# Output projection of a hybrid decoder layer in two parts of K, each by seven half-size products for eight

## The chip, the cores and the metric

The kernel runs on one core of one Trainium2 chip. The metric is the device time of one execution in microseconds. The engines are TensorE (PE; its weight loads are shown apart as PEld), VectorE (DVE), ScalarE (ACT), GpSimd (POOL) and SyncE (SP), whose queue issues every DMA of this kernel.

## The reference

One layer of a hybrid decoder over 2048 tokens and 1024 channels, in float32:

```python
def hybrid_layer(x, g_pre, g_post, w_in, b_i, b_f, g_head, conv_w, g_conv, w_out):
    h = rms_norm(x, g_pre)
    proj = jnp.einsum('bsd,de->bse', h, w_in)
    q, k, v, o, z_m, i_pre, f_pre, u, gate_b, gate_c, z_c = jnp.split(proj, _split_points(), axis=-1)
    ...
    hm = mlstm_chunkwise(qh, kh, vh, log_i, log_f)
    hm = group_rms_norm(hm, g_head, N_MLSTM_HEADS, x.dtype)
    y_m = jax.nn.silu(z_m) * jax.nn.sigmoid(o) * hm
    conv = causal_depthwise_conv(gate_c * u, conv_w)
    y_c = jax.nn.silu(z_c) * group_rms_norm(gate_b * conv, g_conv, N_CONV_GROUPS, x.dtype)
    mix = jnp.concatenate([y_m, y_c], axis=-1)
    out = jnp.einsum('bse,ed->bsd', mix, w_out)
    return x + rms_norm(out, g_post)
```

`mix` has 2048 columns, 1024 of the mLSTM heads and 1024 of the convolution; `w_out` is 2048 x 1024.

## The kernel before

The sequence is worked in two halves (hf = 0, 1) of 1024 tokens. Every float32 matmul is made of three fp32r matmuls: an operand is split into a high part (a cast on ScalarE, line 185) and a remainder (a subtraction on VectorE, line 188).

**Input projections.** The output columns come in 32 pairs of 128-column blocks (`PAIRS`). A pair, times two groups of 512 tokens, times two halves of K (the reduction axis, 2 x 512), is a 2 x 2 by 2 x 2 block product, and `pair` (line 444) does it with seven products instead of eight. Each product is 4 x 3 = 12 matmuls of 128 x 512 (`mm_prod`, lines 296 to 298). The seven right-hand operands of a half ("hops": sums and differences of quarters of the normalised input, each split in two) stay in SBUF; the left-hand ones (sums and differences of weight quarters) stream by. The products accumulate in the PSUM banks X, D and Y; `evac` (line 452) copies X to Y after product 0, and `take` hands the four finished quarters to the stage's own work.

**Slots.** A slot is one product. `on(slot, fn, level)` puts work into a slot; `run_slot` issues it behind the slot's matmuls, in the order of the levels EVAC, WEIGHT, STORE, OTHER, and `in_order` fixes the order of every engine. For a product in slot s the raw weights are loaded in slot s-8, summed on VectorE in s-5, cast on ScalarE in s-4, their remainder taken on VectorE in s-3. The first half ends at slot U = 224, the second at 2U. The mLSTM, convolution and gate work is spread over the same slots.

**Change of operands at U.** During the first half's last block of pairs, `hop_make` computes the second half's operands and stores them in DRAM (`hop_scr`). `plan_fill` (line 1154) then loads them in 14 pieces of 512 KB through four staging tiles (`hop_fill`), and casts and subtracts them into the same SBUF tiles (`hop_high`, `hop_low`) from slot U-6 on, four of the loads from U-10 on. Product j of the new half can only start when its operand is there.

**Output projection.** After slot 2U (first instruction at line 1207) there are no slots. For each of the 16 tiles of 128 tokens the 16 blocks of K are accumulated into two PSUM banks of 512 output columns, with `w_out` in SBUF (28 pieces put into the hop tiles at the end of the second half by `plan_wo`, four more into a pool of their own). The token tile's operand is loaded, multiplied (h from the mLSTM by the gate g, line 1111) and split one tile ahead. The two banks are squared and summed on ScalarE (line 1228), multiplied by `g_post` on VectorE (line 1229), scaled by the row's 1/rms and added to x (line 1238), and stored. The last tile is cut into 512, 256 and 256 columns, done one after the other.

Pools take buffers in turn: a tile that gets the buffer of an earlier one waits for that one's last reader, a DMA too.

Of the kernel before, what the change touches and what calls it, by code (L numbers as in the profile page):

```python
# [29 lines left out]
NPAIR = 32  # L30
NG = NC // 2
# [32 lines left out]
def hybrid_layer_kernel(  # L64
# [54 lines left out]
    w_scr = dram.tile([NPAIR, 4, P, Q], F32, name="w_scr")  # L119

# [90 lines left out]
    def run_slot():  # L211
        while agenda[clock[0]]:
# [227 lines left out]

    def bank_(name):
        return pps.tile([P, Q], F32, tag="pp", name=name)

    def pair(hf, n):
        kind, i = PAIRS[n]
# [3 lines left out]
        def take(ch, qd, src, psum=False):  # L449
            TAKE[kind](hf, i, ch, qd, src, psum)  # L450
# [376 lines left out]
    def hop_fill(m):  # L827
# [4 lines left out]
        nc.sync.dma_start(t, hop_scr[j][:, ks, :])  # L832
        return j, ks, t

    def hop_high(m):
        j, ks, t = S["fill", m]
        if m % 2 == 0:
            S["next", j] = (hop_tile(j, "H", f"hH{j}"), hop_tile(j, "L", f"hL{j}"))
        split_h(S["next", j][0][:, ks], t)

    def hop_low(m):
        j, ks, t = S.pop(("fill", m))
        H, L = S["next", j]
# [3 lines left out]
    def start():  # L847
# [65 lines left out]
        def fill(j, b):  # L913
            H, L = hops[j] = hop_tile(j, "H", f"hH{j}"), hop_tile(j, "L", f"hL{j}")
# [135 lines left out]
    NE = 16  # L1050
    NT = SEQ // P
    wos, ys = {}, {}

    def wo_raw(e, half, raw=None):
        raw = raw or t5("wor")
        nc.sync.dma_start(raw, wout[e * P : (e + 1) * P, seg(half)])
        return raw

    def wo_split(e, half, w2, raw):
        split(w2[:, 0, seg(half)], w2[:, 1, seg(half)], raw)  # L1060
        wos[e] = (w2[:, 0], w2[:, 1])

    def load_wo(e, w2):
        for half in range(2):
            wo_split(e, half, w2, wo_raw(e, half))

    def plan_wo(e):
        s = 2 * U - NPROD + 1 + 3 * e // 4
        j, part = divmod(e, 2)
        R = {}  # L1070

        def load():
            for half in range(2):
                R[half] = wo_raw(e, half, rawp.tile([P, Q], F32, tag="raw", name="wor"))

        def go():
            w2 = hpool.tile([P, 2, DM], F32R, tag=f"h{j}{'HL'[part]}", name="wo")
            for half in range(2):
                wo_split(e, half, w2, R[half])

        on(s - 2, load)
        on(s, go)

    def y_parts(t, tile_):

        hf, tt = divmod(t, NC)
        ts = slice(tt * P, (tt + 1) * P)
        ys[t] = []
        for g in range(2):
            R = {}  # L1090
            for half in range(2):
                es = slice(4 * half, 4 * half + 4)

                def load(g=g, half=half, es=es, R=R):
                    r = R[half] = tpool.tile([P, 4, P], F32, tag="t5", name="yr")
                    if g == 0:
                        for i in range(2):
                            nc.sync.dma_start(
                                r[:, 2 * i : 2 * i + 2, :],
                                h_scr[hf][2 * half + i, tt].rearrange("e p t -> p e t"))  # L1100
                        R["g", half] = tpool.tile([P, 4, P], F32, tag="t5", name="gr")
                        nc.sync.dma_start(R["g", half], g_scr[hf][es, :, ts].rearrange("e p t -> p e t"))
                    else:
                        nc.sync.dma_start(r, y_scr[hf][es, :, ts].rearrange("e p t -> p e t"))

                def go(g=g, half=half, es=es, R=R):
                    if half == 0:
                        R["H"], R["L"] = tile_(f"yH{g}"), tile_(f"yL{g}")
                    r = R[half]
                    if g == 0:  # L1110
                        nc.vector.tensor_tensor(r, r, R["g", half], ALU.mult)
                    split(R["H"][:, es], R["L"][:, es], r)
                    if half == 1:
                        ys[t].extend((R["H"][:, i, :], R["L"][:, i, :]) for i in range(8))

                yield load, go

    def load_y(t, tile_):
        for load, go in y_parts(t, tile_):
            load()  # L1120
            go()

    def even_tile():
        tags = iter(("cv", "cv", "cu", "rb"))
        return lambda name: c4(next(tags), name, [P, 8, P], F32R)

    def y_even(t):
        load_y(t, even_tile())
# [10 lines left out]
    ml = ph1.enter_context(tc.tile_pool(name="ml", bufs=1, reuse_waits="tile"))  # L1139
# [14 lines left out]
    def plan_fill():  # L1154
        for m in range(2 * NPROD):
            s = U - 6 + 11 * m // 14
            early = U - 10 if m < 4 else U - 6 + 11 * (m - 4) // 14 + 2
            def load(m=m):
                S["fill", m] = hop_fill(m)
            on(early, load)  # L1160
            on(s, lambda m=m: hop_high(m))
            on(s + 1, lambda m=m: hop_low(m))

    plan_fill()
    for i, (load, go) in enumerate(y_parts(0, even_tile())):
        on(2 * U - 3 * NPROD + 2 * i, load)
        on(2 * U - 3 * NPROD + 2 * i + 3, go)
    for e in range(2 * NPROD):
        plan_wo(e)
# [4 lines left out]
    class Next(dict):  # L1174
        def __missing__(self, j):
            return S["next", j]

    hops = Next()
    for n in range(NPAIR):
        pair(1, n)  # L1180
        if n == 0:
            for qd, terms in enumerate((((0, 0), (3, 1)), ((0, 0), (4, 0), (6, 1)))):
                bank = gate_proj([(hops[j], lo) for j, lo in terms])
                later(0, lambda qd=qd, bank=bank: gate_take(1, qd, bank))
    while any(agenda.values()):
        run_slot()
    in_order()
    ph1.close()


    def pool2(name, **kw):
        return ctx.enter_context(tc.tile_pool(name=name, reuse_waits="tile", **kw))

    op = pool2("op", bufs=2)
    wo = pool2("wo", bufs=2)
    po = pool2("po", bufs=6, space=PSUM)

    def y_odd(t):
        load_y(t, lambda name: wp.tile([P, 8, P], F32R, tag="w", name=name))

    with tc.high_priority(offset=150):
        for e in range(2 * NPROD, NE):
            load_wo(e, wo.tile([P, 2, DM], F32R, tag="wo", name="wo"))
        y_odd(1)
    gpost = op.tile([P, DM], F32, tag="gpost", name="gpost", bufs=1)
    nc.sync.dma_start(gpost, g_post.broadcast_to([P, DM]))
    for t in range(NT):
        if 0 < t < NT - 1:
            (y_odd if t % 2 == 0 else y_even)(t + 1)
        y2 = ys.pop(t)  # L1210
        xr = op.tile([P, DM], F32, tag="xr", name="xr")
        nc.sync.dma_start(xr, x[t * P : (t + 1) * P, :])
        last = t == NT - 1
        cuts = (0, 512, 768, 1024) if last else (0, 512, 1024)
        parts = [slice(c0, c1) for c0, c1 in zip(cuts, cuts[1:])]
        pts = [po.tile([P, 512], F32, tag="po", name="po")[:, : sl.stop - sl.start] for sl in parts]
        order = [(e, i) for e in range(NE) for i in range(len(parts))]
        if last:
            order.sort(key=lambda ei: ei[1])
# [3 lines left out]
        ot = op.tile([P, DM], F32, tag="ot", name="ot")  # L1223
        junk = op.tile([P, DM], F32, tag="junk", name="junk", bufs=1)
        sss = []
# [67 lines left out]
```

## Time and profile before

| | us |
|---|---|
| median of three runs | 1746.16 |
| lowest and highest run | 1745.42, 1746.17 |
| the profiled execution | 1746.06 |
| its span, first to last instruction | 1744.3 |

The profile is one execution. "Busy" of PE counts a matmul from start to its modelled end, and matmuls overlap; how fast they follow one another is read from their starts. `w` is a split left-hand operand, `wraw` its raw form, `hH` and `hL` the two parts of a right-hand one, `hst` its staging tile, `po` an output bank, `yr` and `yH`, `yL` a token tile and its parts, `ot` the finished rows.

### The profile page before, as it was taken

The page shows a single profiled execution, that of the slowest core. Times are in us where ns is not written, and L with a number is a line of the kernel's source. Part 1 is how long each engine was busy: PE and PEld are TensorE (multiplying, and loading weights), DVE is VectorE, ACT ScalarE, POOL GpSimd, SP SyncE. Part 2 cuts the span into 40 slices and gives each one's busy share as a digit, 9 for nine tenths or more (in the row PEclk, how much of TensorE's full clock was granted, in tenths as well). Part 3 has the DMA queues.
Part 4 walks back from the last instruction along what each step waited for, and adds up shares of the span by engine and source line. Part 5 has one row for each costly group of instructions (what it writes and reads, how often), then busy time and mean ns, then how long its engine had stood idle before and what let it go on. Part 6 is the DMA issues. An engine that isn't in the chain of part 4 may idle for free.

```text
span 1744.3 us, 23010 instructions
## 1 busy us (share of the span) xinstructions
PE 1699.0 (97%) x7773; PEld 1406.4 (81%) x7773; DVE 1152.0 (66%) x2175; ACT 821.4 (47%) x1608; POOL 121.8 (7%) x120
## 2 busy tenths in 40 slices
PE   6799999999999999999999999999999999999998
PEld 4578887888888888788888888888888878888887
DVE  7887669798979888846557777777656753333221
ACT  6244456555656655634445556555656631111110
POOL 5000002010202000000001010102000000000000
PEclk9889999999999999999999999999999999999999
DMA  4177764555455698757774545463556784333310
GB/s 158 50 185 197 186 198 148 159 159 184 150 160 169 210 276 279 247 136 182 177 180 112 160 121 148 106 178 110 154 145 176 235 261 148 120 117 118 110 47 31
DMA packets 360488, 278.40 MB, mean 160 GB/s; under 512 B 188233, under 2 KB 270417, under 8 KB 360370
## 3 DMA queue, kind: packets, MB, share of 16 engines
q1 hardware_dynamic: 360370, 276.93, 55.1%
q8 instruction: 61, 1.00, 0.2%
q14 instruction: 57, 0.47, 0.1%
HBM read 183.25 MB, written 93.59 MB: 159 GB/s over the span
## 4 chain that ended last, share of the span: by engine, by line
PE 87%; DVE 7%; DMA 3%; ACT 1%; issue 1%; SPq 0%; DVEq 0%; ACTq 0%
PE uY L296 9%; PE uY L298 9%; PE uY L297 9%; PE po L624 7%; PE po L623 6%; PE po L625 6%; PE uX L298 6%; PE uX L296 6%; PE uX L297 6%; PE uD L296 6%; PE uD L298 6%; PE uD L297 6%; DMA wor<-in_wout_dram 1%; PE gate L497 1%; PE num L625 1%
## 5 line engine op out<-in xcount | busy, mean ns | idle before, releaser
L185 ACT CAST w<-wraw 128x512 fp32r<-128x512 f32 x410 | 254.2, 621 | 221.0 <-PE uY L298 94.5
L188 DVE TENSOR_TENSOR w<-wraw,w 128x512 fp32r<-128x512 f32 x410 | 279.9, 686 | 81.7 <-ACT w L185 81.4
L296 PE MATMUL uY<-hH,w 128*128 128x512 f32 x744 | 292.6, 393 | 6.9 <-ACT uY L455 4.7
L298 PE MATMUL uY<-hH,w 128*128 128x512 f32 x744 | 290.8, 391 | 0.0
L297 PE MATMUL uY<-hL,w 128*128 128x512 f32 x744 | 290.5, 391 | 0.0
L623 PE MATMUL po<-wo,yH 128*128 128x512 f32 (+1 forms) x528 | 203.3, 385 | 2.2 <-ACT wo L185 2.2
L624 PE MATMUL po<-wo,yH 128*128 128x512 f32 (+1 forms) x528 | 204.5, 387 | 0.2 <-DVE wo L188 0.2
L625 PE MATMUL po<-wo,yL 128*128 128x512 f32 (+1 forms) x528 | 203.1, 385 | 0.0
L296 PE MATMUL uX<-hH,w 128*128 128x512 f32 x496 | 195.4, 394 | 5.0 <-ACT w L185 5.0
L298 PE MATMUL uX<-hH,w 128*128 128x512 f32 x496 | 194.6, 392 | 4.2 <-DVE w L188 4.2
L296 PE MATMUL uD<-hH,w 128*128 128x512 f32 x496 | 194.6, 392 | 0.0
L297 PE MATMUL uX<-hL,w 128*128 128x512 f32 x496 | 194.1, 391 | 0.0
L298 PE MATMUL uD<-hH,w 128*128 128x512 f32 x496 | 193.6, 390 | 0.0
L297 PE MATMUL uD<-hL,w 128*128 128x512 f32 x496 | 193.5, 390 | 0.0
L296 PEld LDWEIGHTS uY<-hH,w 128*128 128x128 f32 x744 | 140.0, 188 | 37.4 <-ACT uY L455 6.1
L298 PEld LDWEIGHTS uY<-hH,w 128*128 128x128 f32 x744 | 140.1, 188 | 29.8
L297 PEld LDWEIGHTS uY<-hL,w 128*128 128x128 f32 x744 | 140.1, 188 | 28.2 <-DVE hL L188 0.2
L623 PEld LDWEIGHTS po<-wo,yH 128*128 128x128 f32 x528 | 99.5, 188 | 23.6 <-ACT wo L185 2.6
L624 PEld LDWEIGHTS po<-wo,yH 128*128 128x128 f32 x528 | 99.6, 189 | 21.2 <-DVE wo L188 1.2
L625 PEld LDWEIGHTS po<-wo,yL 128*128 128x128 f32 x528 | 99.7, 189 | 20.3
L298 PEld LDWEIGHTS uX<-hH,w 128*128 128x128 f32 x496 | 93.6, 189 | 24.8 <-DVE w L188 4.9
L296 PEld LDWEIGHTS uX<-hH,w 128*128 128x128 f32 x496 | 93.8, 189 | 24.2 <-ACT w L185 5.5
(203 smaller groups left out, 2591.0 us busy)
## 6 DMA issues: line engine op xcount, KB each, us to landing
wraw<-in_wt_dram SPq DMA_DIRECT2D x226, 256.0 KB
wraw<-w_scr SPq DMA_DIRECT2D x120, 256.0 KB
w_scr<-wraw SPq DMA_DIRECT2D x90, 256.0 KB
v_scr<-tr SPq DMA_DIRECT2D x128, 64.0 KB
vraw<-v_scr SPq DMA_DIRECT2D x32, 256.0 KB
h_scr<-hT SPq DMA_DIRECT2D x128, 64.0 KB
y_scr<-sg SPq DMA_DIRECT2D x32, 256.0 KB
g_scr<-c SPq DMA_DIRECT2D x32, 256.0 KB
```

The costliest lines, as they stand in the source:

```text
L185: nc.scalar.copy(dH, src)
L188: nc.vector.tensor_tensor(dL, src, dH.bitcast(F32), ALU.subtract)
L296: nc.tensor.matmul(bank, wH[:, k, :], bH[:, k, :], start=first, stop=False, **kw)
L297: nc.tensor.matmul(bank, wH[:, k, :], bL[:, k, :], start=False, stop=False, **kw)
L298: nc.tensor.matmul(bank, wL[:, k, :], bH[:, k, :], start=False, stop=stop and k == KH - 1, **kw)
L497: nc.tensor.matmul(bank, wgt[:, lo * KH + k, :], B[o][:, k, :], start=i == 0, stop=i == len(todo) - 1)
L623: nc.tensor.matmul(out_, aH, bH, start=start, stop=False)
L624: nc.tensor.matmul(out_, aH, bL, start=False, stop=False)
L625: nc.tensor.matmul(out_, aL, bH, start=False, stop=stop)
```

## The change

Each half of K of the output projection, the convolution's 1024 rows of `w_out` first and then the mLSTM's, becomes one "part" (hf = 2 and 3), and each part goes through `pair` like a half of the input projections: eight pairs of token tiles, seven products each, in slots from 2U on. The right-hand operands are now the sums and differences of the quarters of that half of `w_out`, the left-hand ones those of a token tile. A slot schedule therefore covers the whole kernel.

- `wo_make` computes the differences of output weights and stores them in DRAM (`wo_scr`): for the first part in the second half's last block of pairs, for the second during the first part. The fills before slots 2U and 2U + 56 load them, as at U.
- `o_make` multiplies h by the gate for four blocks of a token tile and stores the product in DRAM (`o_scr`): 16 times during the second half (every 10 slots), 16 times from slot 2U + 4 on (every 4 slots).
- The first part's results go to DRAM (`c_scr`); the second part loads them again (`part_load`) and adds them (`row_take`), then does the normalisation, with the 1/rms on GpSimd (`rstd`) instead of ScalarE and VectorE.
- Results of the second part are held in five `ot` buffers of 512 columns, four per pair. Before, an `ot` held 1024 columns, with two buffers.
- The pools `sm`, `rawp`, `pps` and `ps` stay open to the end.

```diff
+    wseq += [(hf, n, j) for hf in (2, 3) for n in range(NOUT) for j in range(NPROD)]
+    def y_quarter(pas, t, half):
+        src = (y_scr, o_scr)[pas][t // NC]
+        return src[4 * half : 4 * half + 4, :, t % NC * P : (t % NC + 1) * P].rearrange("e p t -> p e t")
...
+    def part_store(n, ch, qd, src, psum):
+        store(c_scr[2 * n + ch][:, seg(qd)], in_sbuf(src, psum))
+    def part_load(n, ch, qd):
+        S["pc", ch, qd] = t5("pc")
+        nc.sync.dma_start(S["pc", ch, qd], c_scr[2 * n + ch][:, seg(qd)])
+    def row_take(n, ch, qd, src, psum):
+        t = 2 * n + ch
+        last = n == NOUT - 1 and ch == 0
+        o = S["ot", t, qd] = op.tile([P, Q], F32, tag="ot", name="ot", bufs=5)
+        nc.vector.tensor_tensor(o, src, S.pop(("pc", ch, qd)), ALU.add)
+        def square():
+            ss = op.tile([P, 1], F32, tag=f"oss{qd}", name="oss")
+            nc.scalar.activation(t5("junk"), o, AF.Square, accum_out=ss)
+            S.setdefault(("oss", t), []).append(ss)
+            if len(S["oss", t]) == 1 + (n < NOUT - 1):
+                S["xr", t] = op.tile([P, DM], F32, tag="xr", name="xr")
+                nc.sync.dma_start(S["xr", t], x[t * P : (t + 1) * P, :])
+            if len(S["oss", t]) == 2:
+                later(0 if last else 1, lambda: row_rstd(t, last))
+        def scale():
+            nc.vector.tensor_tensor(o, o, S["gpost"][:, seg(qd)], ALU.mult)
+        if last and qd == 1:
+            square()
+            scale()
+        else:
+            later(1, square)
+            later(2, scale)
+    def row_rstd(t, last):
+        a, b = S.pop(("oss", t))
+        nc.vector.tensor_tensor(a, a, b, ALU.add)
+        rstd(a, 1.0 / DM)
+        later(0 if last else 2, lambda: row_out(t, a, last))
+    def row_out(t, r, last):
+        xr = S.pop(("xr", t))
+        for qd in range(2):
+            o, dst = S.pop(("ot", t, qd)), out[t * P : (t + 1) * P, seg(qd)]
+            nc.vector.scalar_tensor_tensor(o, o, r, xr[:, seg(qd)], ALU.mult, ALU.add)
+            store(dst, o, 0 if last else 1)
...
-            mm_prod(b, wops.pop((hf, n, j)), hops[j], j < 2, True)
+            mm_prod(b, wops.pop((hf, n, j)), hops[hf, j], j < 2, True)
...
+    def hop_source(pas, j):
+        if pas == 1:
+            return hop_scr[j]
+        half, ch = {0: (0, 0), 3: (1, 0), 6: (1, 1)}.get(j, (None, None))
+        if half is None:
+            return wo_scr[pas - 2][j]
+        r = WOUT0[pas - 2] + half * KH * P
+        return wout[r : r + KH * P, seg(ch)].rearrange("(e p) c -> p e c", p=P)
...
+        for p, s in enumerate((U + OZ0, 2 * U)):
+            for d, fn in wo_make(p, k):
+                on(s + 10 + 9 * k + d, fn)
+    for i in range(2 * NT):
+        for d, fn in o_make(*divmod(i, 2)):
+            on((U + 40 + 10 * i if i < NT else 2 * U + 4 + 4 * (i - NT)) + d, fn)
...
+    OUT = NOUT * NPROD
+    for pas, end in ((1, U), (2, 2 * U), (3, 2 * U + OUT)):
+        plan_fill(pas, end)
...
+    for n in range(NOUT):
+        s = 2 * U + OUT + n * NPROD
+        for d, ch, qd in ((1, 0, 0), (2, 1, 1), (3, 1, 0), (4, 0, 1)):
+            on(s + d, lambda n=n, ch=ch, qd=qd: part_load(n, ch, qd))
+    for pas in (2, 3):
+        for n in range(NOUT):
+            pair(pas, n)
...
-    for t in range(NT):
-        if 0 < t < NT - 1:
-            (y_odd if t % 2 == 0 else y_even)(t + 1)
...
-        for e, i in order:
-            w2 = (wos[e][0][:, parts[i]], wos[e][1][:, parts[i]])
-            mm3(pts[i], y2[e], w2, e == 0, e == NE - 1)
```

VectorE in the output projection, kernel before: the work on one token tile, in the middle of the stage.

```order
L1111 TENSOR_TENSOR yr<-yr,gr 128x512
L188 TENSOR_TENSOR yL_15297<-yr,yH_15296 128x512 x2
L1111 TENSOR_TENSOR yr<-yr,gr 128x512
L188 TENSOR_TENSOR yL_15312<-yr,yH_15311 128x512
L1229 TENSOR_TENSOR ot<-po,gpost 128x512 x2
L1232 TENSOR_TENSOR oss<-oss 128x1
L188 TENSOR_TENSOR yL_15312<-yr,yH_15311 128x512
L1235 RECIPROCAL oss<-oss 128x1
L1238 SCALAR_TENSOR_TENSOR ot<-ot,oss,xr 128x1024
```

VectorE in the second part of the change, from the fourth slot of a pair on: `uX`, `uY` and `uD` are PSUM banks, `pc` the first part's results, `p` and `u2` copies of banks, line 191 the remainders, lines 247 and 271 sums of token tiles.

```order
L461 TENSOR_TENSOR ot_16192<-uX_16074,pc_16121 128x512
L191 TENSOR_TENSOR w_16172<-wraw_16068,w_16172 128x512
L271 TENSOR_TENSOR wraw_16093<-wraw_16093,wraw_16119 128x512
L247 TENSOR_TENSOR wraw_16068<-wraw_16093,wraw_16068 128x512
L493 SCALAR_TENSOR_TENSOR ot_16012<-ot_16012,oss_16046,xr_16127 128x512
L493 SCALAR_TENSOR_TENSOR ot_16088<-ot_16088,oss_16046,xr_16127 128x512
L527 TENSOR_TENSOR c22_16217<-p_16144,uY_16113 128x512
L461 TENSOR_TENSOR ot_16219<-c22_16217,pc_16151 128x512
L191 TENSOR_TENSOR w_16195<-s3_16174,w_16195 128x512
L531 TENSOR_TENSOR c21_16241<-u2_16169,uD_16075 128x512
L461 TENSOR_TENSOR ot_16243<-c21_16241,pc_16176 128x512
L191 TENSOR_TENSOR w_16222<-wraw_16068,w_16222 128x512
```

The tile `ot_16219` takes the buffer of `ot_16012`, the fifth before it, whose last writer stands three rows above; the remainders of the next products now stand behind that row.

VectorE at the end of the kernel, before: the last token tile.

```order
L1229 TENSOR_TENSOR ot<-po,gpost 128x512
L1229 TENSOR_TENSOR ot<-po,gpost 128x256
L1232 TENSOR_TENSOR oss<-oss 128x1
L1229 TENSOR_TENSOR ot<-po,gpost 128x256
L1232 TENSOR_TENSOR oss<-oss 128x1
L1235 RECIPROCAL oss<-oss 128x1
L1238 SCALAR_TENSOR_TENSOR ot<-ot,oss,xr 128x512
L1238 SCALAR_TENSOR_TENSOR ot<-ot,oss,xr 128x256 x2
```

And in the change, from the last bank's addition on; `ot_16360` and `ot_16413` are the even row tile, `ot_16382` and `ot_16405` the odd one.

```order
L461 TENSOR_TENSOR ot_16413<-uY_16289,pc_16364 128x512
L474 TENSOR_TENSOR ot_16413<-ot_16413,gpost_13642 128x512
L474 TENSOR_TENSOR ot_16382<-ot_16382,gpost_13642 128x512
L485 TENSOR_TENSOR oss_16386<-oss_16386,oss_16415 128x1
L493 SCALAR_TENSOR_TENSOR ot_16360<-ot_16360,oss_16386,xr_16389 128x512
L493 SCALAR_TENSOR_TENSOR ot_16413<-ot_16413,oss_16386,xr_16389 128x512
L474 TENSOR_TENSOR ot_16405<-ot_16405,gpost_13642 128x512
L485 TENSOR_TENSOR oss_16408<-oss_16408,oss_16420 128x1
L493 SCALAR_TENSOR_TENSOR ot_16405<-ot_16405,oss_16408,xr_16411 128x512
L493 SCALAR_TENSOR_TENSOR ot_16382<-ot_16382,oss_16408,xr_16411 128x512
```

Two row tiles are finished after the last product instead of one, one behind the other.

SP's DMA issues while operands are exchanged, from the fifth staged load on, in the kernel before (at U):

```order
L832 DMA hst_6930<-hop_scr_82 128x1024
L832 DMA hst_6932<-hop_scr_82 128x1024
L209 DMA h_scr0_62<-hT_6925 32x16x32 x4
L832 DMA hst_6962<-hop_scr_82 128x1024
L832 DMA hst_6986<-hop_scr_82 128x1024
L231 DMA wraw_7005<-in_wt_dram 128x512
L832 DMA hst_7009<-hop_scr_82 128x1024
L832 DMA hst_7011<-hop_scr_82 128x1024
```

And in the change, between its two parts:

```order
L903 DMA hst_14888<-wo_scr1_87 128x1024
L903 DMA hst_14890<-wo_scr1_87 128x1024
L903 DMA hst_14916<-in_wout_dram 128x2x512
L212 DMA c_scr_88<-cs_14904 128x512
L903 DMA hst_14941<-in_wout_dram 128x2x512
L240 DMA wraw_14960<-o_scr0_84 128x4x128
L212 DMA c_scr_88<-c22_14930 128x512
L903 DMA hst_14966<-wo_scr1_87 128x1024
L903 DMA hst_14968<-wo_scr1_87 128x1024
L240 DMA wraw_14989<-o_scr0_84 128x4x128
L212 DMA c_scr_88<-c21_14955 128x512
L212 DMA o_scr1_85<-yh_14881 128x4x128
```

Stores of partial sums and of mLSTM outputs now stand between the staged loads.

## Rows read from the trace of the kernel before

**Rows 1.** The page: span, and busy us of each engine (share, instructions)

```profile
span 1744.3 us, 23010 instructions
PE 1699.0 (97%) x7773; PEld 1406.4 (81%) x7773; DVE 1152.0 (66%) x2175; ACT 821.4 (47%) x1608; POOL 121.8 (7%) x120
```

**Rows 2.** Table by stage: us, PE, PEld, DVE, ACT, POOL busy, PEclk, DMA share, GB/s

```profile
540.00:700.00 160.00, 159.16 (x747) 132.75 (x746) 138.85 (x264) 94.63 (x186) 10.14 (x11) 1.00 0.80 251
675.00:700.00 25.00, 25.00 (x120) 21.01 (x119) 20.45 (x38) 12.91 (x26) 1.04 (x2) 1.00 0.86 296
700.00:735.00 35.00, 32.92 (x144) 26.48 (x144) 33.60 (x45) 24.33 (x37) 0.00 (x0) 1.00 0.77 249
...
1404.00:1720.00 316.00, 316.00 (x1382) 259.06 (x1381) 94.86 (x159) 56.21 (x132) 0.00 (x0) 1.00 0.40 121
```

**Rows 3.** Groups by shape, 1380 to 1745 us: busy us, mean ns, idle before

```profile
L624 PE MATMUL po<-wo,yH 128*128 128x512 f32 x496 | 195.5, 394 | 0.2 <-DVE wo L188 0.2
...
L624 PE MATMUL po<-wo,yH 128*128 128x256 f32 x32 | 9.0, 282 | 0.0
```

**Rows 4.** Timeline of PE, 1361 to 1382 us: start, duration, instruction

```profile
1361.57 0.39 PE L296 MATMUL uX<-hH,w 128*128 128x512 f32 x1
...
1377.66 0.39 PE L298 MATMUL uD<-hH,w 128*128 128x512 f32 x1
...
1381.18 0.39 PE L623 MATMUL po<-wo,yH 128*128 128x512 f32 x1
```

**Rows 5.** Timeline of PE at U and near 1223 us, with idle before

```profile
720.02 0.50 PE L296 MATMUL uY<-hH,w 128*128 128x512 f32 x1 [1.01 <-ACT uY L455]
...
732.27 0.47 PE L296 MATMUL uY<-hH,w 128*128 128x512 f32 x1 [1.07 <-DVE c L466]
...
1223.46 0.50 PE L296 MATMUL uY<-hH,w 128*128 128x512 f32 x1 [1.71 <-ACT uY L455]
```

**Rows 6.** Waits, 695 to 735 us: total us, times, longest us

```profile
ACT hH L185 <- DMA hst<-hop_scr: 8.9, 5, 2.5
```

**Rows 7.** Chain that ended last: start, us, what

```profile
82.28 1.95 DMA kt_scr<-tr
...
591.60 0.60 DVE w L188
592.20 0.60 DVE wraw L238
...
1392.24 6.36 DMA wor<-in_wout_dram
```

**Rows 8.** Timeline, 1735 to 1745 us

```profile
1737.84 0.28 PE L625 MATMUL po<-wo,yL 128*128 128x256 f32 x1
1738.16 0.38 ACT L1228 ACTIVATE junk<-po 128x256 f32<-128x256 f32 x1 [5.26 <-PE po L625]
...
1739.72 1.54 DVE L1238 SCALAR_TENSOR_TENSOR ot<-ot,oss,xr 128x512 f32<-128x512 f32 x3
```

**Rows 9.** Groups by shape, 1380 to 1745 us; lines 412 and 413: ns min/median/max

```profile
L1228 ACT ACTIVATE junk<-po 128x512 f32<-128x512 f32 x31 | 18.6, 599 | 147.9 <-PE po L625 147.9
L1228 ACT ACTIVATION_READ_ACCUMULATOR junk<-po 128x1 f32 x33 | 6.4, 195 | 0.0
L1238 DVE SCALAR_TENSOR_TENSOR ot<-ot,oss,xr 128x512 f32<-128x512 f32 x1 | 0.8, 752 | 0.0
...
L412 POOL TENSOR_SCALAR hss<-hss x32: 191/296/1788, 199.8 to 1353.0; 128x2 f32<-128x2 f32 x32
...
L413 POOL TENSOR_TENSOR hss<-hss,mhalf x32: 695/755/1149, 200.3 to 1353.3; 128x2 f32<-128x2 f32 x32
```

**Rows 10.** Timeline of POOL and DVE, 283 to 290 us

```profile
284.46 2.90 POOL L413 TENSOR_TENSOR red<-red,mhalf 128x16 f32<-128x16 f32 x1
...
286.29 0.68 DVE L238 TENSOR_TENSOR s<-wraw 128x512 f32<-128x512 f32 x1
286.89 0.68 DVE L188 TENSOR_TENSOR w<-wraw,w 128x512 fp32r<-128x512 f32 x1
```

More of the change, by code (lines that the diff above doesn't have):

```diff
@@ L119, in hybrid_layer_kernel @@
     w_scr = dram.tile([NPAIR, 4, P, Q], F32, name="w_scr")
+    o_scr = scratch("o_scr", [8, P, HT])
+    wo_scr = [dram.tile([NPROD, P, KH, Q], F32, name=f"wo_scr{i}") for i in range(2)]
+    c_scr = dram.tile([NT, P, DM], F32, name="c_scr")
     eps = const.tile([P, 1], F32, name="eps")
@@ L831, in hop_fill, with hop_high, hop_low @@
         ks = slice(2 * half, 2 * half + 2)
-        nc.sync.dma_start(t, hop_scr[j][:, ks, :])
+        nc.sync.dma_start(t, hop_source(pas, j)[:, ks, :])
         return j, ks, t
-    def hop_high(m):
-        j, ks, t = S["fill", m]
+    def hop_high(pas, m):
+        j, ks, t = S["fill", pas, m]
         if m % 2 == 0:
[L838 to L843, printed above, removed]
+            hops[pas, j] = (hop_tile(j, "H", f"hH{j}"), hop_tile(j, "L", f"hL{j}"))
+        split_h(hops[pas, j][0][:, ks], t)
+    def hop_low(pas, m):
+        j, ks, t = S.pop(("fill", pas, m))
+        H, L = hops[pas, j]
         split_l(H[:, ks], L[:, ks], t)
@@ L1047, in start @@
         assert clock[0] == NSTART
[L1050 to L1069, printed above, removed]
+    WOUT0 = (HT, 0)
@@ L1070, in plan_wo, with wo_make @@
+    def wo_make(p, k):
         R = {}
         def load():
[L1073 to L1084, printed above, removed]
-        hf, tt = divmod(t, NC)
[L1087 to L1128, printed above, removed]
+            R["a"], R["b"] = c4("cv", "woa"), c4("cv", "wob")
+            for half, key in enumerate("ab"):
+                r = WOUT0[p] + (half * KH + k) * P
+                nc.sync.dma_start(R[key], wout[r : r + P, :])
@@ new lines, in put, with first, second @@
+        def put(j, t):
+            store(wo_scr[p][j][:, k, :], t)
+        def first():
+            B0, B1, B3 = R["a"][:, seg(0)], R["a"][:, seg(1)], R["b"][:, seg(1)]
+            R["t"] = c4("cu", "woT12", [P, 2, Q])
+            T1, T2 = R["t"][:, 0], R["t"][:, 1]
+            sub(T1, B1, B0)
+            sub(T2, B3, T1)
+            put(4, T1)
+            put(2, T2)
+        def second():
+            B1, B2, B3 = R["a"][:, seg(1)], R["b"][:, seg(0)], R["b"][:, seg(1)]
+            t = c4("rb", "woT34", [P, 2, Q])
+            sub(t[:, 0], B3, B1)
+            sub(t[:, 1], B2, R["t"][:, 1])
+            put(1, t[:, 0])
+            put(5, t[:, 1])
@@ new lines, in wo_make, with o_make, load, mult @@
+        return (0, load), (4, first), (6, second)
+    def o_make(t, half):
+        hf, tt = divmod(t, NC)
+        es, ts = slice(4 * half, 4 * half + 4), slice(tt * P, (tt + 1) * P)
+        R = {}
+        view = lambda a: a.rearrange("p (e t) -> p e t", t=P)
+        def load():
+            R["h"], R["g"] = t5("yh"), t5("yg")
+            for i in range(2):
+                nc.sync.dma_start(
+                    view(R["h"])[:, 2 * i : 2 * i + 2, :], h_scr[hf][2 * half + i, tt].rearrange("e p t -> p e t"))
+            nc.sync.dma_start(view(R["g"]), g_scr[hf][es, :, ts].rearrange("e p t -> p e t"))
+        def mult():
+            nc.vector.tensor_tensor(R["h"], R["h"], R["g"], ALU.mult)
+            store(o_scr[hf][es, :, ts].rearrange("e p t -> p e t"), view(R["h"]))
+        return (0, load), (3, mult)
@@ L1182, in hybrid_layer_kernel @@
             for qd, terms in enumerate((((0, 0), (3, 1)), ((0, 0), (4, 0), (6, 1)))):
-                bank = gate_proj([(hops[j], lo) for j, lo in terms])
+                bank = gate_proj([(hops[1, j], lo) for j, lo in terms])
                 later(0, lambda qd=qd, bank=bank: gate_take(1, qd, bank))
+    mlx.close()
+    op = ctx.enter_context(tc.tile_pool(name="op", bufs=2, reuse_waits="tile"))
+    S["gpost"] = op.tile([P, DM], F32, tag="gpost", name="gpost", bufs=1)
+    nc.sync.dma_start(S["gpost"], g_post.broadcast_to([P, DM]))
```

95 lines of the change are left out of this document (24 added, 71 removed).

## Prediction

> **What bounds the kernel now.** The page comes first: TensorE is busy 97% of the span, VectorE 66%, ScalarE 47% [rows 1]. A busy share alone does not say that TensorE sets the pace, so I read next the table by stage. In the output projection, 1404 to 1720 us, TensorE is busy for all 316 us while VectorE has work for 95, ScalarE for 56, and the DMA engines run at a share of 0.40 [rows 2]. There, only fewer matmuls can save time. In the stretches ahead of it TensorE is as full, but VectorE and the DMA engines are close behind: 160 us at a DMA share of 0.80, and 33.6 of 35 us of VectorE where one half of the sequence hands over to the other [rows 2].
>
> The groups by shape give the stage's size. Each of the three output lines has 496 matmuls of 512 columns and 32 of 256, so 1488 and 96 [rows 3]. Their mean duration of 390 ns is no price, since they overlap. The price is the distance of starts: in the input products the matmuls at 1361.57 and 1377.66 are 71 steps apart, 226.6 ns each [rows 4]; in the output stage 1382 matmuls fill 316 us, 228.7 ns each [rows 2]. The output stage begins at 1381.18 [rows 4], its last matmul ends at 1737.84 + 0.28 = 1738.12, and the span at 1744.3 [rows 8, 1]: 356.9 us of stage and 6.2 of tail. The profiled execution took 1746.06 us, 1.8 more than its span and 0.1 under the median of the three runs, so the sum needs no correction.
>
> **The products.** The change replaces 1536 matmuls' worth of columns by 2 parts x 8 pairs of token tiles x 7 products x 12 = 1344 matmuls of 512 columns, of the same form as the input products and on the same banks. Their price lies between 226.6 ns (304.5 us) and 228.7 ns (307.4); I take 227.7, since weights are loaded and copied beside them as in both stretches: 306.0 us. TensorE's order up to 1381.18 is unchanged, so the new stage starts there, later only by what is put into the second half.
>
> In the Trainium skill, "TensorE: Matmul & The Clock Gate", section "Wait — 56ns, not 53.3ns?", gives 215.7 ns from start to start for 512 columns at full clock; by it these products would take 289.9 us and the end come 16 us earlier. The trace does not agree: 226.6 ns is its even step at a granted clock of 1.00 [rows 4, 2], so I give that time no chance.
>
> **Work added to the second half.** VectorE gets 14 products h*g and 16 differences of output weights before 1381. At 0.60 us from start to start [rows 7] that is 18 us spread over some 600, in a stage in which TensorE hardly waits; the one wait of note there is 1.71 us at 1223.46, behind a copy on ScalarE [rows 5]. The SP queue gets their loads and stores. TensorE covers all of it; I put 0.5 us for one wait that grows (0 to 2; I see nothing that gains).
>
> **The boundaries.** The new stage has two places at which all seven right-hand operands are exchanged while products run, at its start and between its two parts. The trace has one: between the two halves of the sequence TensorE waited 1.01 and 1.07 us [rows 5], and behind it ScalarE waited 8.9 us in all for the staged operand [rows 6]. Price: 2.1 us where the queues are as full as there. At the new stage's start they nearly are: I take 2.5 (0 to 4.6). The 9.2 us of gate matmuls that follow the first pair in the trace's case, and let VectorE catch up, are missing here.
>
> Between the parts they are fuller. In SP's order the last ten staged loads (10 x 512 KB = 5.24 MB) have beside them, in the trace's case, four weight loads, a store of 256 KB and four of 64 KB, 6.8 MB in all; in the change four loads of token tiles, four stores of partial sums, a complete set h, g and o of mLSTM outputs and two loads of partial sums, 8.6 MB. The 1.8 MB more take 6 us at 296 GB/s, the most that a window shows [rows 2]. So 2.1 to 8.3 us; without any wait, if the queue runs ahead, 0. I take 5.
>
> **First part, between the boundaries.** Beside 4 loads and 4 stores of 256 KB per pair, 16 sets of h, g and o (12.6 MB) and the second part's weight differences (8.4 MB) pass the SP queue and the DMA engines. With the 8.4 MB each of y and partial sums and 7.3 staged, this part moves some 45 MB in 153 us, 295 GB/s: about the 296 GB/s that the trace reached for 25 us at a share of 0.86, and above the 251 that it held for 160 us at 0.80 [rows 2]. Loads stand three slots (8 us) ahead of their use, against up to 6.36 us for one load on the chain [rows 7]; I put 1.5 us (0 to 9: 45 MB at 251 GB/s would be 26 us more than the part lasts, but some is done early and the second part, at 34 MB, lets the rest pass).
>
> **Second part.** Per pair VectorE has 7 remainders, 4 sums of y, 2 combined quarters, 4 additions of the partial sum and 4 multiplications by g_post: 21 x 0.60 = 12.6 us; 4 final operations at 0.75 = 3.0; two small sums 0.3: 15.9 us [rows 7, 9]. The pair lasts 84 x 0.2277 = 19.1. There is one new wait: the addition for quarter (1,1) takes the fifth buffer of `ot` after the one of the pair before, and that one's store has only just been issued; behind the waiting addition stand the remainders of the next products, which TensorE needs three slots later. After the final operation that frees the store, VectorE has 0.75 + 0.60 us of other work. A store costs 1.95 us (64 KB) to 6.36 (a load of 256 KB under load) [rows 7]; the nearest row is the end of the kernel, where the last final operations end by 1741.3 and the span 3.0 later [rows 8, 1]. At 3.0 the wait is 1.7 us and VectorE's sum 17.6, below 19.1. So nothing reaches TensorE: 0.
>
> "SBUF — State Buffer", section "SBUF: two separate sides", in the Trainium skill says that a GpSimd operation and a VectorE operation with two SBUF inputs exclude each other. GpSimd gets two small operations per row tile here, 0.30 + 0.76 us [rows 9]; by the rule 2.1 us per pair. The trace speaks against it: under a GpSimd operation from 284.46 for 2.90 us, VectorE's two-input operations start at 286.29 and 286.89, the usual 0.60 apart and 0.68 long [rows 10].
>
> **The tail.** Before, the last tile's columns are finished in three pieces, and 6.2 us follow the last matmul. Now, counted from that end: addition out of PSUM 0.7; square and its readout 0.7 [rows 9]; the multiplication in place must wait for the square, and another one stands behind it, 1.3; small sum 0.15; GpSimd 1.05; two final operations 1.5: 5.4 us for the even row tile. Behind them, in VectorE's order, the odd row tile has a multiplication 0.7, sum 0.15, GpSimd 1.05 and two final operations 1.5: 8.9; the store 3.0. Sum 11.9 us (10 to 14).
>
> **Sum.** 1381.2 + 0.5 + 306.0 + 2.5 + 1.5 + 5.0 + 0.2 (the last matmul's run-out) = 1696.9; + 11.9 = 1708.8; + 1.8 = 1710.6 us. Forecast 1711, 35 us below before: 50.9 saved on the stage's 356.9, less 9.7 for the waits and the run-out, less 5.7 at the end.
>
> **Rivals.**
> - TensorE never waits: the queue runs ahead, as in stretches where DMA shares were near 0.86 and TensorE was busy 25 of 25 us [rows 2]. 1381.2 + 304.5 + 0.2 + 11.9 + 1.8 = 1700. Against it: the waits of the one known boundary.
> - The `ot` ring makes VectorE the bound of the second part. At 6.36 us for the store, the wait is 5.0 and the pair 20.9 us of VectorE, 1.8 over 19.1 in seven pairs: 13 us, 1724. For it: the queue has 8.4 MB each of y, partial sums, x and out in this part; against it: the part's 34 MB in 153 us are 222 GB/s, below what the trace carried without trouble.
> - Slower than before: the DMA engines become the bound of the whole stage. Both parts move 79 MB where the stage before moved 121 GB/s x 357 us = 43. To end at 1746 the stage may last 1746.2 - 1.8 - 11.9 - 1381.2 = 351 us, which is 225 GB/s: below that it is slower, at 200 GB/s 395 us, so 1790. For it: token tiles and o are read and written in pieces of 512 bytes, and the trace never held more than 251 GB/s for long. Against it: at 251 it had a share of 0.80 only.
> - The exclusion of GpSimd and VectorE: 17.6 + 2.1 = 19.7 us per pair against 19.1, 0.6 x 8 = 5 us, 1716.
>
> **How the numbers follow.** Forecast 0.63, no waits 0.15, `ot` ring 0.13, exclusion 0.04, DMA-bound 0.05. What a measurement can tell from no change is 0.2%, 3.5 us; only the DMA rival comes near or past it, and 0.01 of the rest I leave for a tie: faster 0.94, same 0.01, slower 0.05. The forecast's own bounds (waits 0 to 24, tail 10 to 14) and the first two rivals give 1699 to 1727.
>
> **What would show it.** In the new profile: product starts 0.227 us apart from 1381 on, 1344 of them; idle TensorE of 2 to 3 us within the first ten slots after 1381 and of some 5 us at about 1535 to 1555, released by ScalarE or VectorE behind staged operands; a wait of VectorE for a store of `ot` once per pair, without an idle TensorE; DMA shares near 0.9 until the second part; 12 us from the last matmul to the end. Wrong would be: idle TensorE in every pair of the second part, a first part stretched as a whole, or input products that end later than 1383.

## The result and the profile after

The changed kernel takes 1705.9 us (median of four runs, 1704.58 to 1707.94) against 1746.16 before (four runs by now, 1745.42 to 1747.16): a ratio of 0.977 with a 95% interval of 0.9753 to 0.9787. The profiled execution took 1707.94 us, of which its span is 1706.2; it was the longest of the four, so the terms below add up to a time 2 us above the median.

The page of the changed kernel: span; busy us of each engine; DMA share in tenths and GB/s in 40 slices of 42.7 us.

```profile
span 1706.2 us, 23384 instructions
...
PE 1653.8 (97%) x7533; PEld 1368.6 (80%) x7533; DVE 1291.8 (76%) x2375; ACT 887.9 (52%) x1697; POOL 139.6 (8%) x152
...
DMA  4177774546454788856876565556587788899774
GB/s 157 51 186 189 187 186 156 181 133 209 124 168 131 236 260 262 286 140 163 220 192 170 151 190 155 175 151 177 158 235 243 238 254 264 258 302 296 232 234 155
```

Against [rows 1], TensorE has 240 matmuls fewer (7773 to 7533: the 1584 of the old stage, 96 of them of 256 columns, give way to 1344) and 45 us less of busy time at the same share. The other engines have more work, and the end of the span, where DMA engines ran at 30 to 40%, is now the part in which they are fullest.

The table by stage of the changed kernel, with columns as in [rows 2]: the exchange of operands at the start of the first part, the rest of that part in two pieces, the exchange between the parts, the second part.

```profile
1383.00:1404.00 21.00, 19.05 (x81) 14.48 (x80) 19.04 (x25) 13.72 (x21) 0.00 (x0) 1.00 0.92 286
1404.00:1490.00 86.00, 86.00 (x381) 71.22 (x380) 50.22 (x79) 31.50 (x56) 0.00 (x0) 1.00 0.86 268
1490.00:1535.00 45.00, 45.00 (x200) 37.25 (x200) 30.69 (x45) 22.08 (x35) 0.00 (x0) 1.00 0.91 287
1535.00:1560.00 25.00, 21.83 (x91) 17.64 (x90) 21.00 (x28) 14.75 (x23) 0.00 (x0) 0.93 1.06 349
1560.00:1694.00 134.00, 134.00 (x593) 110.80 (x592) 110.59 (x188) 55.87 (x122) 16.81 (x28) 1.00 0.68 220
```

TensorE is full in three of the five rows, at DMA shares up to 0.91 and beside a VectorE that works 110.59 of 134 us. It waits in the other two, the exchanges. Where, shows the timeline of PE: the first matmuls of pairs 0, 1 and 2 of the first part and of pairs 0 and 1 of the second, the last matmul, and the five with an idle time ahead of them.

```profile
1381.72 0.39 PE L305 MATMUL uX<-hH,w 128*128 128x512 f32 x1
...
1387.68 0.50 PE L305 MATMUL uY<-hH,w 128*128 128x512 f32 x1 [0.36 <-ACT uY L516]
...
1394.17 0.50 PE L305 MATMUL uY<-hH,w 128*128 128x512 f32 x1 [0.71 <-ACT u L522]
...
1400.33 0.47 PE L305 MATMUL uY<-hH,w 128*128 128x512 f32 x1 [0.41 <-DVE c L527]
...
1402.64 0.50 PE L306 MATMUL uY<-hL,w 128*128 128x512 f32 x1 [0.48 <-DVE hL L191]
...
1403.90 0.40 PE L305 MATMUL uX<-hH,w 128*128 128x512 f32 x1
...
1422.95 0.39 PE L305 MATMUL uX<-hH,w 128*128 128x512 f32 x1
...
1537.19 0.39 PE L305 MATMUL uX<-hH,w 128*128 128x512 f32 x1
...
1551.41 0.79 PE L305 MATMUL uY<-hH,w 128*128 128x512 f32 x1 [3.17 <-ACT u L522]
...
1561.05 0.39 PE L305 MATMUL uX<-hH,w 128*128 128x512 f32 x1
...
1694.20 0.39 PE L307 MATMUL uY<-hH,w 128*128 128x512 f32 x1
```

Pair 1 lasts from 1403.90 to 1422.95, 19.05 us: 84 matmuls 226.7 ns apart, the step of [rows 4] (226.6). Pairs 2 to 7 last as long (114.24 us for six). A pair without a wait thus takes 19.04 us, called even below. Pair 0 of the first part lasts 22.18, 3.1 longer; pair 0 of the second 23.86, 4.8 longer. Of these 4.8, 3.3 are the gap ahead of 1551.41 (the start before it would have been followed 0.227 later); the rest, some 1.5, is lost behind it. There the granted clock is at the lower of its two levels, after a stretch in which TensorE started nothing for 3.57 us: 0.93 in the mean of that window, and of the first seven steps behind the gap one takes 0.59 us, five some 0.427 and one 0.32, instead of 0.227. The waits behind the gap, 1535 to 1560 us, as total us, times, longest us:

```profile
ACT hH L188 <- DMA hst<-wo_scr: 5.8, 3, 4.1
...
PE uY L305 <- ACT u L522: 3.2, 1, 3.2
ACT hH L188 <- DMA hst<-in_wout_dram: 2.8, 3, 1.5
```

That is [rows 6] again at another place: ScalarE stands at the cast of a staged operand until its load has landed, and the copy that frees a bank for TensorE stands behind it. SP's queue shows why the load is late. The cast that waited longest starts at 1547.08, and its load was issued at 1540.32, behind the store of one set h*g and the loads of the next:

```profile
1537.34 0.37 SPq L212 DMA_DIRECT2D o_scr<-yh  x1
...
1540.32 1.61 SPq L903 DMA_DIRECT2D hst<-wo_scr  x1
```

The end of the kernel, lines of DVE, ACT and POOL, answering to [rows 8]:

```profile
1694.63 0.69 DVE L461 TENSOR_TENSOR ot<-uY,pc 128x512 f32<-128x512 f32 x1 [0.63 <-PE uY L307]
...
1696.03 0.61 ACT L465 ACTIVATE junk<-ot 128x512 f32<-128x512 f32 x1
1696.16 1.29 DVE L474 TENSOR_TENSOR ot<-ot,gpost 128x512 f32<-128x512 f32 x2 [0.84 <-ACT junk L465]
...
1697.68 0.19 POOL L421 TENSOR_SCALAR oss<-oss 128x1 f32<-128x1 f32 x1 [15.62 <-DVE oss L485]
1697.96 0.54 POOL L422 TENSOR_TENSOR oss<-oss,mhalf 128x1 f32<-128x1 f32 x1
1698.53 1.41 DVE L493 SCALAR_TENSOR_TENSOR ot<-ot,oss,xr 128x512 f32<-128x512 f32 x2 [1.01 <-POOL oss L422]
...
1701.62 1.41 DVE L493 SCALAR_TENSOR_TENSOR ot<-ot,oss,xr 128x512 f32<-128x512 f32 x2 [1.01 <-POOL oss L422]
```

From the last matmul's end at 1694.6 to the span's end 11.6 us pass, against 6.2 before; the two row tiles follow one another, as read from the order.

### The profile page after: what moved, and what is told of

It reads as the page before. It is cut to its first block, busy times and chain, and to the rows that moved or that the text cites. A ratio compares the mean times of both kernels' runs of the same rounds, so it can differ in the third digit from the quotient of the medians.

```text
span 1706.2 us, 23384 instructions
## 1 busy us (share of the span) xinstructions
PE 1653.8 (97%) x7533; PEld 1368.6 (80%) x7533; DVE 1291.8 (76%) x2375; ACT 887.9 (52%) x1697; POOL 139.6 (8%) x152
## 5 line engine op out<-in xcount | busy, mean ns | idle before, releaser
L188 ACT CAST w<-wraw 128x512 fp32r<-128x512 f32 x506 | 313.8, 622 | 278.6 <-PE uY L307 105.9
L191 DVE TENSOR_TENSOR w<-wraw,w 128x512 fp32r<-128x512 f32 x506 | 345.8, 686 | 120.0 <-ACT w L188 116.9
L305 PE MATMUL uY<-hH,w 128*128 128x512 f32 x936 | 368.3, 393 | 11.9 <-ACT uY L516 5.7
L306 PE MATMUL uY<-hL,w 128*128 128x512 f32 x936 | 365.7, 391 | 0.5 <-DVE hL L191 0.5
L307 PE MATMUL uY<-hH,w 128*128 128x512 f32 x936 | 366.2, 391 | 0.0
L305 PE MATMUL uX<-hH,w 128*128 128x512 f32 x624 | 245.5, 393 | 5.0 <-ACT w L188 5.0
L307 PE MATMUL uX<-hH,w 128*128 128x512 f32 x624 | 244.4, 392 | 4.2 <-DVE w L191 4.2
L305 PE MATMUL uD<-hH,w 128*128 128x512 f32 x624 | 244.5, 392 | 0.0
L307 PE MATMUL uD<-hH,w 128*128 128x512 f32 x624 | 243.6, 390 | 0.0
L305 PEld LDWEIGHTS uY<-hH,w 128*128 128x128 f32 x936 | 176.4, 188 | 51.2 <-ACT uY L516 7.5
L307 PEld LDWEIGHTS uY<-hH,w 128*128 128x128 f32 x936 | 176.2, 188 | 37.5
L307 PEld LDWEIGHTS uD<-hH,w 128*128 128x128 f32 x624 | 117.2, 188 | 25.0
L306 PEld LDWEIGHTS uX<-hL,w 128*128 128x128 f32 x624 | 117.9, 189 | 24.0
L306 PEld LDWEIGHTS uD<-hL,w 128*128 128x128 f32 x624 | 117.4, 188 | 23.8
L305 PEld LDWEIGHTS uD<-hH,w 128*128 128x128 f32 x624 | 117.4, 188 | 23.5
```

The lines of the kernel that those rows point to most:

```text
L188: nc.scalar.copy(dH, src)
L191: nc.vector.tensor_tensor(dL, src, dH.bitcast(F32), ALU.subtract)
L305: nc.tensor.matmul(bank, wH[:, k, :], bH[:, k, :], start=first, stop=False, **kw)
L306: nc.tensor.matmul(bank, wH[:, k, :], bL[:, k, :], start=False, stop=False, **kw)
L307: nc.tensor.matmul(bank, wL[:, k, :], bH[:, k, :], start=False, stop=stop and k == KH - 1, **kw)
```

## The experiments

Each is an edit of the changed kernel. The first four ran on one chip, the last four on another, without the unedited changed kernel beside them; all are compared with the kernel before on their own chip, whose medians were 1744.68 and 1745.22 us. Ratios are to that kernel, with a 95% interval.

**The changed kernel again.**

> The changed kernel again, unedited, as the measure for the others on the same chip. All theories: 1705 to 1708 us; TensorE waits about 5 us between the two parts, 3 us at the start of the first, and 11.6 us follow the last matmul.

1706.37 us (1705.25 to 1707.34), ratio 0.9778 (0.9765 to 0.9792). Pair 0 of the first part lasts 22.25 us, that of the second 23.96. This run is the control for the others.

**The eighth product given back.**

```diff
+            if hf > 1 and j == 0:
+                mm_prod(b, wops[hf, n, j], hops[hf, j], True, True)
             mm_prod(b, wops.pop((hf, n, j)), hops[hf, j], j < 2, True)
```

> In every pair of both parts product 0 is issued twice (the second run overwrites the first), so 8 x 12 matmuls per pair as with a plain block product: 192 more. Theory (the gain is the number of matmuls at an unchanged step): 192 x 0.2267 = 43.5 us more than the changed kernel, less up to 5 for the waits at the boundaries, since the first slots of a pair last longer: 1744 to 1750. Rival (the gain comes from the slots, the pools kept open and the order, not from the count): under 1730.

1744.85 us, ratio 0.9999 (0.9989 to 1.0008): the kernel before, to within a tenth of a per cent. That is 38.5 us above the control. The 192 matmuls cost 43.5 at the even step; 4.9 come back at the exchanges, where the long first slots let the loads arrive: with eight products an even pair takes 21.76 us, and the two pairs 0 last 22.96 and 23.83. The longest idle times of PE there, at the start of the first part:

```profile
1401.07 0.47 PE L305 MATMUL uY<-hH,w 128*128 128x512 f32 x1 [0.37 <-DVE c L527]
```

and between the parts:

```profile
1571.54 0.50 PE L305 MATMUL uY<-hH,w 128*128 128x512 f32 x1 [1.07 <-ACT u L522]
```

So everything else in the change (slots to the end, scratch tensors, the new end) nets to nothing, and the gain goes with the product left out. That the rest nets to nothing is a coincidence of two sums. The old stage took 356.9 us, 8.7 more than its 1536 matmuls' worth of columns would at 226.7 ns (348.2). The edited kernel saves these 8.7, and loses 3.3 at its two exchanges and 5.4 at its longer end (11.6 us against 6.2).

**Six sets moved out of the exchange.**

```diff
-            on((U + 40 + 10 * i if i < NT else 2 * U + 4 + 4 * (i - NT)) + d, fn)
+            on((U + 40 + 10 * i if i < NT else 2 * U + (4 if i < NT + 10 else 24) + 4 * (i - NT)) + d, fn)
```

> The last six of the sixteen sets h*g of the second half are moved from slots 2U+44 to 2U+64 to slots 2U+64 to 2U+84, out of the exchange of operands between the parts. Theory A (the wait there is the price of bytes that share the queue): 0.8 MB less beside the staged loads and 2.4 MB less in the slots ahead, at 0.3 MB per us: the wait falls from 4.8 to 2 to 3 us, the time by 2 to 3. Rival B (a staged load may only be issued one slot ahead of its use, since four staging tiles turn, and takes longer than that whatever else runs): wait and time unchanged within 1 us.

Pair 0 of the second part lasts 19.99 us, just under 1 above the even 19.04 where the control has 4.9: more than theory A had promised, and against B. The idle times of PE in this exchange are now

```profile
1547.56 0.50 PE L305 MATMUL uY<-hH,w 128*128 128x512 f32 x1 [0.17 <-ACT u L522]
...
1555.06 0.50 PE L306 MATMUL uY<-hL,w 128*128 128x512 f32 x1 [0.18 <-DVE hL L191]
```

With the gap, the clock's fall goes too: the granted clock of this window is 1.00. The load whose cast waited longest above is issued at 1537.03 and cast at 1543.29:

```profile
1537.03 0.32 SPq L903 DMA_DIRECT2D hst<-wo_scr  x1
...
1543.29 1.05 ACT L188 CAST hH<-hst 128x1024 fp32r<-128x1024 f32 x1 [1.08 <-DMA hst<-wo_scr]
```

From issue to cast it takes 6.3 us, in the profile after 6.8. Counted from the pair's first matmul, the cast comes 2.9 us earlier, and 2.4 of these are the earlier issue. So the sets delayed the staged load above all by standing ahead of it in SP's order.

The profiled executions differ by 3.0 us (spans 1705.6 and 1702.6), the medians by 1.2 only (1706.37 and 1705.15; ratio 0.9772, 0.9759 to 0.9786): the intervals overlap, so by the times alone this edit is not told from none. Of the 4 us in the traces, 1.1 are lost again at the very end: from VectorE's last operation to the end of the span 4.3 us pass, against 3.2 in the control. Why, these runs don't show.

**The last pair in another order.**

```diff
+        if n == NOUT - 1 and (ch, qd) == (1, 1):
+            square()
+            later(1, scale)
+        elif n == NOUT - 1 and ch == 1:
+            square()
+            def first():
+                scale()
+                S["r1"] = row_root(t)
+            later(0, first)
+        elif last and qd == 1:
+            square()
+            row_half(t + 1, 1, S["r1"])
+            r = row_root(t)
+            scale()
+            row_half(t + 1, 0, S["r1"])
+            row_half(t, 0, r)
+            row_half(t, 1, r)
...
```

`row_root` is the sum and `rstd`, `row_half` the final operation and the store of one half.

> In the last pair the odd row tile, whose quarters come before the last product, is normalised first, its square and 1/rms ahead of the last bank's addition, and its two final operations lie between those of the even tile. Theory (the 11.6 us at the end are a chain of two row tiles one behind the other on VectorE and GpSimd): the chain from the last matmul falls to about 8 us, the time by 3 to 4. Rival (the end is set by the stores and the end of the program): less than 1 us.

1703.81 us (1701.39 to 1705.12), ratio 0.9764 (0.9751 to 0.9777), 2.6 below the control where 3 to 4 were expected. The two intervals overlap, so it is the trace that tells the effect. Its end:

```profile
1690.25 0.39 PE L307 MATMUL uY<-hH,w 128*128 128x512 f32 x1
...
1691.23 0.69 DVE L461 TENSOR_TENSOR ot<-uY,pc 128x512 f32<-128x512 f32 x1
...
1693.88 0.93 POOL L422 TENSOR_TENSOR oss<-oss,mhalf 128x1 f32<-128x1 f32 x1
1694.84 1.42 DVE L506 SCALAR_TENSOR_TENSOR ot<-ot,oss,xr 128x512 f32<-128x512 f32 x2 [0.43 <-POOL oss L422]
```

The last matmul ends at 1690.64 and the span at 1699.4: 8.8 us against 11.6. The last bank's addition starts 0.6 us after that matmul, since the odd tile's multiplication and sum stand ahead of it; without that the end would come to an estimated 8.2, the "about 8" of the theory.

**The bytes of the sets without the sets.** With the six sets moved, loads of the same size go into buffers that nobody reads.

```diff
+    def dummy(k):
+        a, b = (op.tile([P, DM], F32, tag="xr", name="dummy") for _ in range(2))
+        for i, t in enumerate((a[:, :Q], a[:, Q:], b[:, :Q])):
+            nc.sync.dma_start(t.rearrange("p (e t) -> p e t", t=P), y_quarter(0, k, i % 2))
+    for k in range(6):
+        on(2 * U + 44 + 4 * k, lambda k=k: dummy(k))
```

> As the run with the six sets moved, but in their old slots (2U+44 to 2U+64) three loads of 256 KB each, in pieces of 512 bytes, go into buffers that nobody reads: the bytes of a set without its multiplication and without anybody waiting for it. Theory A (bytes on the queue delay the staged loads): the wait between the parts comes back from 0.9 to 3 to 5 us, the time to that of the changed kernel or 1 us above. Rival C (VectorE, which stands at the multiplication until its set has landed): the wait stays under 1.5 us.

The wait is back: pair 0 of the second part lasts 24.43 us, 5.4 above even, and the waits at 1535 to 1560 us are like those of the unedited kernel.

```profile
ACT hH L188 <- DMA hst<-wo_scr: 5.1, 3, 3.3
...
ACT hH L188 <- DMA hst<-in_wout_dram: 4.5, 4, 2.6
...
PE uY L305 <- ACT u L522: 3.5, 1, 3.5
```

1708.79 us, ratio 0.9789 (0.9776 to 0.9802); 4.7 MB more pass the queue in all. No computation waits for the dummy loads, and VectorE's work is the moved one, so rival C falls: what passes the queue beside the staged loads is what delays them. Whether it does so by its bytes or by its place in SP's order is not separated: the dummy loads bring as many bytes as the sets' loads and stores did, and they stand in the same queue.

**Every token-tile load of the first part twice.**

```diff
+            if hf == 2 and clock[0] >= 2 * U:
+                t = op.tile([P, DM], F32, tag="xr", name="twice")
+                nc.sync.dma_start(t[:, :Q].rearrange("p (e t) -> p e t", t=P), y_quarter(0, 2 * n + q // 2, q % 2))
```

> In the first part every token-tile load is issued twice, the second time into a buffer that nobody reads: 8 MB more in 153 us on top of 268 to 287 GB/s. Theory A (TensorE is at the edge of the DMA engines there): the stretch needs 325 GB/s, more than the 300 or so that this trace held; TensorE waits inside the pairs of the first part, 5 to 20 us in all. Rival (room is left): pairs 1 to 7 stay at 19.04 us each and only the boundary between the parts grows, by under 3 us.

Theory A falls here. The second loads begin at slot 2U: 27 of them, 7.1 MB, issued from 1381.7 to 1506.1 us. The table by stage of this run:

```profile
1383.00:1404.00 21.00, 17.47 (x69) 13.61 (x68) 17.65 (x22) 13.89 (x21) 0.00 (x0) 0.92 1.01 324
1404.00:1490.00 86.00, 86.00 (x381) 71.23 (x380) 50.65 (x80) 30.55 (x55) 0.00 (x0) 1.00 1.02 308
1490.00:1535.00 45.00, 45.00 (x201) 37.24 (x200) 28.39 (x43) 19.78 (x33) 0.00 (x0) 1.00 1.04 323
1535.00:1560.00 25.00, 20.89 (x85) 16.52 (x84) 20.92 (x28) 16.44 (x23) 0.00 (x0) 0.93 1.04 351
```

At a DMA share of 1.02 to 1.04 and 308 to 323 GB/s, pairs 1 to 7 of the first part still last 19.04 us each. Both exchanges lose more (pair 0: 24.79 and 25.11 us), the first too, which the rival had left out: 5.8 us above even against 3.2 in the control. The time is 1708.33 us (1707.67 to 1711.45), ratio 0.979 (0.9777 to 0.9803).

**Both helpful edits.**

> Both edits that helped, the six sets moved and the new end of the last pair. Theory (two separate places, so they add): wait between the parts about 1 us, end about 8.8 us, 4 us below the changed kernel: 1701 to 1703. Rival (they share a cause): no better than the new end alone, 1704.

1701.18 us (1700.34 to 1702.5), ratio 0.9746 (0.9733 to 0.9759), as the theory expected. Its interval lies clear of the control's, which that of neither single edit does. By the ratios the two together save 5.6 us, alone 1.0 and 2.4: that they add fits this within the intervals, and is not shown more closely. In the trace pair 0 of the second part is 1.4 us above even, and 9.8 us follow the last matmul, each more than the expected 1 and 8.8.

**And six staging tiles between the parts.**

```diff
-        t = c4(STAGE[m % 4], "hst", [P, 2, Q])
+        if pas == 3 and m % 6 > 3:
+            t = op.tile([P, DM], F32, tag="xr", name="hst").rearrange("p (a b) -> p a b", b=Q)
+        else:
+            t = c4(STAGE[m % (6 if pas == 3 else 4)], "hst", [P, 2, Q])
...
+            if pas == 3 and m > 3:
+                early = end - 9 if m < 6 else end - 6 + 11 * (m - 6) // 14 + 2
```

> As the run before, and the exchange between the parts is staged through six tiles instead of four (two buffers of the later x tiles), so that a staged load is issued up to three slots ahead instead of one. If the rest of the wait between the parts is the short lead: another 0.9 us, 1700 to 1702. If not: the same as the run before within 0.5 us.

1700.02 us (1698.63 to 1700.72), ratio 0.9737 (0.9723 to 0.975), the lowest median of these kernels, 2.6% below before. Its interval overlaps that of the run before, so here too the trace decides: pair 0 of the second part lasts 19.22 us instead of 20.48, and that the rest of the wait was the short lead holds. ScalarE no longer waits for a staged operand between the parts, and TensorE is full there:

```profile
1535.00:1560.00 25.00, 25.00 (x111) 20.45 (x111) 23.76 (x33) 16.33 (x28) 0.00 (x0) 1.00 0.96 317
```

## Why the prediction was right, and where not

The time, 1705.9, lies in the range 1699 to 1727 and 5 us under the forecast of 1711. By its own steps, on the profiled execution of 1707.94, where the misses of the terms (-1.4, +0.6, -1.5, -0.2 and -0.3 us) nearly all point one way and add up to about the 2.7 by which the sum, 1710.6, was too high; the median lies 2 us lower still:

- **The products.** Forecast 306.0 us at 227.7 ns; the sixteen pairs at their even 19.04 us are 304.6, the lower of the two bounds. The step of the old output stage, 228.7, was not taken over. That the count makes the gain was argued, and the eighth product given back shows it, with the rest of the change cancelling as told there.
- **Work added to the second half.** Start expected at 1381.7, found at 1381.72. The hit is luck: in the kernel before it was 1381.18 [rows 4], and in the profiles of the nine runs of the changed kernel and its edits, whose order up to there is the same, it lies between 1378.73 and 1381.72. No run shows the 0.5 us of this term.
- **The first exchange.** 2.5 forecast, 3.1 found, in four small gaps. The doubled loads, which make it 5.8, show that what passes the queue beside the staged loads counts here too; a longer lead was not tried here.
- **The rest of the first part.** 1.5 forecast, 0 found. The step that failed is the reading that a stretch at 295 GB/s must lose something because the trace before had held only 251 GB/s for long; the doubled loads show room to 323.
- **The exchange between the parts.** 5 forecast, 4.8 found, and in the main for the forecast's reason: loads of the sets' size, put back without the sets, bring the wait back. But the hit on the number is in part luck. Some 1.5 us of it are lost behind the gap, mostly to the lower clock, which the forecast had not counted; the transport, priced at 5, was 3.3. And the forecast took it for bytes at a rate, where the trace shows a load that is issued late.
- **The `ot` ring.** Its term of 0 was right and its reason wrong. The rival rested on buffers taken strictly in turn, which the text on the kernel states too: that the addition for (1,1) takes the buffer of the pair before's (0,0). In the built program `ot_16219` has the address of `ot_16063`, which is (1,0) of the odd tile, and not that of `ot_16012`: it waits for that tile's store, two stores earlier. The timeline agrees: VectorE and the stores of a pair in the second part,

```profile
1627.04 1.00 SPq L212 DMA_DIRECT2D out_dram<-ot  x2
...
1631.89 1.41 DVE L493 SCALAR_TENSOR_TENSOR ot<-ot,oss,xr 128x512 f32<-128x512 f32 x2
...
1632.66 1.00 SPq L212 DMA_DIRECT2D out_dram<-ot  x2
...
1633.21 0.68 DVE L527 TENSOR_TENSOR c<-p,uY 128x512 f32<-128x512 f32 x1
...
1633.93 0.69 DVE L461 TENSOR_TENSOR ot<-c,pc 128x512 f32<-128x512 f32 x1
```

  where the addition at 1633.93 follows its operand `c` in 0.72 us, as the next one does without a store near it, and 6.9 us after the store of the odd tile was issued. The wait that the rival priced at 5 us could not have come.
- **VectorE in the second part.** 15.9 us per pair forecast; 110.59 us in 134 are 15.7 per 19.04.
- **The tail.** 11.9 forecast (its terms add up to 11.8), 11.6 found, and by its steps: the even row tile is done after 5.3 us (5.4 forecast), the odd one after 8.4 (8.9), the span ends 3.2 later (3.0). The new order of the last pair moves it as such a chain should.
- **Slower, bound by the DMA engines.** The first part moved 268 GB/s or more in each row of the table by stage, against the 225 below which this rival would have won; the doubled loads put the bound above 308.

## What to carry to other kernels

When TensorE is full and its matmuls follow at an even step, count matmuls and multiply by the distance of starts: that step held up to a DMA share of 1.04 beside it. What such a change gives back, look for at the few places where operands are exchanged with a short lead; list what the queue's order puts beside and ahead of the staged loads, and move what nobody needs yet. And read from the program, not from the number of buffers, which earlier tile a buffer was.

## What the runs showed of the hardware

TensorE's step of 226.7 ns did not change up to a DMA share of 1.04 (the share is taken over 16 engines, and over 25 us it reached 1.06 at 349 GB/s). And GpSimd's small operations take longer beside some of VectorE's, though VectorE's do not beside them. In the second part, with VectorE at work on operations with two inputs in SBUF:

```profile
1641.37 0.69 DVE L191 TENSOR_TENSOR w<-wraw,w 128x512 fp32r<-128x512 f32 x1
...
1641.59 0.52 POOL L421 TENSOR_SCALAR oss<-oss 128x1 f32<-128x1 f32 x1 [16.65 <-DVE oss L485]
...
1641.99 0.69 DVE L474 TENSOR_TENSOR ot<-ot,gpost 128x512 f32<-128x512 f32 x1
...
1642.19 0.88 POOL L422 TENSOR_TENSOR oss<-oss,mhalf 128x1 f32<-128x1 f32 x1
```

they take 0.52 and 0.88 us; at the end, with VectorE idle, 0.19 and 0.54. Beside VectorE's addition out of PSUM they take 0.19 and 0.54 too (the last pair in another order, 1691.48 and 1691.75 us). VectorE's two-input operations start 0.62 us apart meanwhile, about as always. In these rows VectorE's operation is under way first; that VectorE isn't held by a GpSimd operation under way either, [rows 10] show. So the exclusion that the Trainium skill's "SBUF — State Buffer", section "SBUF: two separate sides", states shows here on GpSimd's side alone, and the rival built on it (5 us) did not come.
